# Output projection of a decoder layer as seven products of halves, on one Trainium2 core

## The chip, the core and the metric

The kernel runs on one core of a Trainium2 chip. A core has five engines with a queue of instructions each: TensorE (PE) multiplies matrices and writes to the accumulators (PSUM), VectorE (DVE) and ScalarE (ACT) work on elements, GpSimd (POOL) does so too and issues those transfers that add to their target, SyncE (SP) issues the plain loads. Each engine takes its queue in the order in which the program was built; semaphores make one engine wait for another or for a transfer. The metric is the time of one execution in device microseconds (us), as a median of several runs.

## The reference

Two decoder layers work on a stream x of 512 tokens by 1024 channels in float32. Only what the change touches is spelled out:

```python
for l in range(2):
    x = x + 0.5 * swiglu(rms_norm(x, g1[l]), wg1[l], wu1[l], wd1[l])
    h = rms_norm(x, gmix[l])
    z = h @ w_in[l]                       # q | k | v | conv_B | conv_C | conv_h
    attn_out = sliding_window_attention(q, k, v, sink[l])      # 512 x 512
    conv_out = conv_B * causal_conv3(conv_C * conv_h)          # 512 x 512
    x = x + concat([attn_out, conv_out]) @ w_out[l]            # 1024 x 1024
    x = x + 0.5 * swiglu(rms_norm(x, g2[l]), wg2[l], wu2[l], wd2[l])
return rms_norm(x, gfinal)
```

## The kernel before, in words

The stream lies transposed in four pairs of tiles (`xpair`, `xs`): 128 channels on the partitions, 512 tokens along each row. A float32 product is made of three products in a shorter float type: each operand is split into a high part, cast by ACT (`split`, line 198), and a low part, subtracted by DVE (line 199), and PE adds high x high, high x low and low x high.

Weights come through one list of units (`plan`, `add_unit`). A unit is a tile of 128 x 1024 float32 values, 512 KB. `need_raw` has SP load it (line 182) into one of 8 "raw" slots, which attention shares for its probabilities, and has POOL add a second block to it on the way in where the unit is a sum (line 193). `need_split` makes the high and low parts two groups ahead, in three buffers each. With "far" as the way (lines 236 to 238), ACT makes both the high part and a negated copy, and a transfer issued by POOL adds the raw tile to the copy, so DVE has nothing to do.

In most of the feed-forward the products run in a scheme of seven products of halves instead of eight (`seven` for the weights, `CHAINS`, `SHARES` and the class `Seven` for the operand): the weight matrix and the operand are cut in two by two, sums of the blocks are formed (the operand's are called b11, b21, t2, t3, t1, t4, b22), and seven products of half size give the result. The down projection has two such stages per feed-forward ("s"); `share` runs each: seven steps of two groups, 48 products of 128x256 per step (`stand`), and after each step two updates of a quarter of the stream on DVE (line 892). Where a norm follows, `take_half` (lines 407 to 435) makes its operands by quarters, after steps 3, 4, 5 and 6.

`mix` is the part of the layer between the feed-forwards. Eighteen groups of `w_in` give k, v, q and the conv inputs; between the groups, `attend` runs eight units of attention (scores, softmax, transposes, values). Attention results are added up by DVE (line 1217), cast by ACT (line 1221) and their low part is subtracted by POOL (line 1222); conv results are multiplied by POOL (line 1272), cast by ACT (1273), and their low part subtracted by DVE (1274). Then come eight groups of 24 products of 128x512 with `w_out` (lines 1278 to 1281), each added to one tile of the stream (1280) and handed to the next norm (`after`, lines 387 to 405).

A planner sets the order of the work on each engine when the program is built, outside the opening; the order is fixed from then on.

Of the kernel before, what the change touches and what calls it, by code (L numbers as in the profile page):

```python
# [58 lines left out]
def trunk_kernel(  # L59
# [55 lines left out]
    def f32(ap):  # L115
        return ap.bitcast(F32)
# [84 lines left out]
    def need_split(g):  # L201
        while state["split"] <= min(g, len(order) - 1):
# [3 lines left out]
            if what in (None, "wide", "far"):  # L206
                need_raw(u + LOAD_AHEAD)
                raw = raw_of.pop(u)
            elif isinstance(what, tuple):

                what, h, how = what
                far = how == "far"
                last = {"a11": 0, "a12": 4, "s2": 2, "s3": 6, "s1": 2, "a22": 8, "s4": 4}[what]
                need_raw(u + max(last, 4) + h + LOAD_AHEAD)
                a11, s1, a12, s3, a22 = (raw_of.get(u + 2 * i + h) for i in range(5))
                if what == "s2":
                    nc.vector.tensor_add(a11, a11, s1)  # L217
                raw = {"a11": a11, "a12": a12, "s2": a11, "s3": s3, "s1": s1, "a22": a22, "s4": a12}[what]
            else:

                need_raw(u + 4 + LOAD_AHEAD)
                a11, a12, s1, s3, a22 = (raw_of.get(u + i) for i in range(5))
                if what == "s2":
                    nc.vector.tensor_add(a11, a11, s1)
                if what == "s4":
                    nc.vector.tensor_add(a11, a11, a12)
                raw = {"a11": a11, "a12": a12, "s2": a11, "s3": s3, "s1": s1, "a22": a22, "s4": a11}[what]
                if what == FORMS[-1]:
                    for i in range(5):
                        del raw_of[u + i]  # L230
# [417 lines left out]
    def make_bias():  # L648
# [9 lines left out]
        for h in range(NH):  # L658
            nc.vector.scalar_tensor_tensor(
                bias[:, h, :], df, -(2.0 ** -(h + 1)), m0, op0=ALU.mult, op1=ALU.add  # L660
            )


    def ffn(norm, stages, after=None, late=None):

# [167 lines left out]

            pending.extend(lambda *tag, c=c: turn(c, *tag) for c in range(NT))

        def stand(accs, wh, wl, xh, xl, h, start):

            for c in range(4):
                cols = slice(c * P, (c + 1) * P)
                for k in range(2):  # L840
                    for i, (w, x_) in enumerate(((wh, xh), (wh, xl), (wl, xh))):

                        nc.tensor.matmul(  # L843
                            accs[c // 2][:, c % 2, :],
                            w[:, k, cols],
                            x_[:, 2 * h + k, :],
                            start=start and c % 2 == 0 and h + k + i == 0,
                            stop=h + k == 2 and i == 2,
                            skip_group_check=True,
                        )  # L850

        def stream(accs, wh, wl, xh, xl, h, start):

            for u in range(2):
                tok = slice(u * P, (u + 1) * P)
                for k in range(2):
                    for i, (x_, w) in enumerate(((xh, wh), (xl, wh), (xh, wl))):
                        nc.tensor.matmul(  # L858
                            accs[u],
                            x_[:, 2 * h + k, tok],  # L860
                            w[:, k, :],
                            start=start and h + k + i == 0,
                            stop=h + k == 2 and i == 2,
                            skip_group_check=not start,
                        )

        def share(b, ops, between, y=None):


            accs = {}  # L870
            for step, (acc, operand, start) in enumerate(CHAINS):
                ops.make(operand)
                xh, xl = ops.forms[operand]
                if start:
                    tag = {"x": "mm", "y": "sc", "w": "aux"}[acc]
                    shape = [P, 2, H] if y is None else [P, S]
                    accs[acc] = [psum(tag, shape, f"{acc}_{ops.name}_{m}") for m in range(2)]
                o, t, sign = SHARES[step]
                for h in range(2):
                    _, wh, wl = take_split()  # L880
                    if y is None:
                        stand(accs[acc], wh, wl, xh, xl, h, start)
                    else:
                        stream(accs[acc], wh, wl, xh, xl, h, start)
                    if h == 0:
                        continue
                    for m in range(2):
                        if y is None:
                            part = xpair[2 * o + m][:, :, t * H : (t + 1) * H]
                        else:  # L890
                            part = y[2 * t + m][o]
                        nc.vector.scalar_tensor_tensor(
                            part, accs[acc][m], 0.5 * sign, part, op0=ALU.mult, op1=ALU.add
                        )
                if step < 3:
                    ops.make(CHAINS[step + 4][1])
                between(step)

        def shared(b):
            return Seven([raws[b], raws[b + 2]], room_form, f"s_{norm.i}_{b}")  # L900

        def turns(step):
# [2 lines left out]
                flush()  # L905
            if step == 2:
                flush(2, "mm")

        def ahead(ops, at):
            return lambda step: ops.make(*at.get(step, ()))  # L910

        sevens = [b for what, b in stages if what == "s"]
        blocks = [b + j for b in sevens for j in (0, 2)]
# [9 lines left out]
        for i, (what, b) in enumerate(stages):  # L923
# [10 lines left out]
            if what == "s" and b == sevens[0]:  # L934
                then = shared(sevens[1])
                share(
                    b,
                    ops,
                    ahead(then, {3: ("b11",), 4: ("b21",), 5: ("t2",), 6: ("t3",)}),
                    end and end.y,  # L940
                )
            elif what == "s" and i + 1 == len(stages):
                share(b, then, after.step)
            elif what == "s":
                share(b, then, lambda step: 2 <= step < 6 and flush(1, "aux"), end and end.y)
            if what == "p":
                plain(b)
                if b == 0 and late:
# [146 lines left out]


    def mix(l, norm, after):
        mixed = [None] * KC
        q = [None] * NH

        def scaled(acc, name, by=None):
            t = g2(name)
# [11 lines left out]
        for g in range(NKV):  # L1114
# [5 lines left out]
        amix = {}  # L1120
        for g in range(NKV):
            h = parts_of(f"m_{l}_{g}")
            amix[g] = h
            for j in range(2):
                mixed[2 * g + j] = (h[0][:, j, :], h[1][:, j, :])

        def take_values():
            vf = scaled(vacc, f"vf_{l}")
# [13 lines left out]
        class Unit:  # L1142
# [61 lines left out]
            def values(self):  # L1204
# [7 lines left out]
                    nc.tensor.matmul(o, v, lo, start=False, stop=i == len(self.pt) - 1)  # L1212
# [8 lines left out]
                nc.scalar.copy(mh, f)  # L1221
                nc.gpsimd.tensor_sub(ml, f, f32(mh))

        todo = [Unit(n, g) for g in range(NKV) for n in range(NT)]

# [21 lines left out]
        for pair in range(2):  # L1247
# [6 lines left out]
            for j in range(2):  # L1254
# [11 lines left out]
                ys.append(y)  # L1266
                attend(step)
                step += 1
            hi, lo = parts_of(f"m_{l}_{2 + pair}")
            for j in range(2):  # L1270
                b = scaled(group(norm.h), f"cb_{l}_{pair}_{j}")
                nc.gpsimd.tensor_mul(b, b, ys[j])
                nc.scalar.copy(hi[:, j, :], b)
                nc.vector.tensor_sub(lo[:, j, :], b, f32(hi[:, j, :]))
                mixed[4 + 2 * pair + j] = (hi[:, j, :], lo[:, j, :])
# [62 lines left out]
```

## Time and profile before

| | |
|---|---|
| median of 3 runs | 1692.73 us (1692.41 to 1692.82) |
| the profiled execution | 1692.13 us, its span 1690.3 us |
| granted TensorE clock | 0.999 |
| PE busy | 1680.5 us, 99% of the span |
| DVE busy | 1345.3 us, 80% |
| ACT busy | 942.3 us, 56% |
| POOL busy | 209.5 us, 12% |
| projection of layer 0 | 470.2 to 513.7 us |

Times in the views are us from the start of the span, if not marked ns. A row of the timeline has the start, the duration, the engine, the line of the kernel, the operation, output <- inputs, the shape, the number of instructions merged, and in brackets how long the engine was idle before and what ended that. Durations overlap: an engine starts the next instruction before the last has left, so what an instruction costs a full queue is the distance from start to start. In the table by stretch each engine's busy time is followed by its number of instructions.

### The profile page before, as it was taken

What the parts mean: (1) busy time and instruction counts of PE and PEld (TensorE: products, weight loads), DVE (VectorE), ACT (ScalarE), POOL (GpSimd) and SP (SyncE); (2) the same over time, 40 slices, a digit from 0 to 9 for tenths busy, and PEclk for the clock granted to TensorE, in tenths of its full rate; (3) what the DMA queues carried; (4) which work ended last, traced back from release to release, by engine and by line L of the source; (5) the groups of instructions that cost most, each with busy time, mean ns of one, the idle gap of its engine ahead of it and who ended that gap; (6) DMA issues with size and microseconds to landing.
All of it is one profiled execution on the core that took longest, in us unless ns stands there. A gap on an engine that the chain in (4) does not pass through costs nothing.

```text
span 1690.3 us, 22800 instructions
## 1 busy us (share of the span) xinstructions
PE 1680.5 (99%) x8726; PEld 1434.4 (85%) x8726; DVE 1345.3 (80%) x1751; ACT 942.3 (56%) x1309; POOL 209.5 (12%) x190
## 2 busy tenths in 40 slices
PE   9999999999999999999999999999999999999998
PEld 6888899988888888889988888999888888888886
DVE  7987679988858976799798777997787597667995
ACT  6545565466535655564465555644565466556654
POOL 1011111001211111111011111110023011111111
PEclk9999999999999999999999999999999999999999
DMA  8467777731337677778576777794223457777881
GB/s 250 104 170 190 185 198 184 191 100 51 112 102 154 172 183 182 186 195 209 163 150 170 191 185 184 192 224 139 62 63 114 112 124 192 184 185 185 222 215 50
DMA packets 197600, 271.53 MB, mean 161 GB/s; under 512 B 8620, under 2 KB 91636, under 8 KB 197492
## 3 DMA queue, kind: packets, MB, share of 16 engines
q1 hardware_dynamic: 162308, 197.85, 37.5%
q0 software_dynamic: 34032, 70.79, 24.7%
q8 instruction: 68, 1.11, 0.3%
q10 hardware_dynamic: 1152, 1.45, 0.2%
q14 instruction: 40, 0.33, 0.1%
HBM read 254.85 MB, written 2.10 MB: 152 GB/s over the span
## 4 chain that ended last, share of the span: by engine, by line
PE 96%; DVE 2%; ACT 1%; DMA 0%; issue 0%; SPq 0%; ACTq 0%; DVEq 0%
PE x L858 24%; PE y L858 12%; PE acc L271 9%; PE acc L268 9%; PE acc L275 9%; PE x_s L843 8%; PE w L858 6%; PE y_s L843 4%; PE x_s L858 3%; PE w_s L843 2%; PE at L823 2%; PE y_s L858 1%; PE x L737 1%; PE w_s L858 1%; PE pt L1197 1%; DVE p L1190 0%
## 5 line engine op out<-in xcount | busy, mean ns | idle before, releaser
L198 ACT CAST wh<-raw 128x1024 fp32r<-128x1024 f32 (+1 forms) x472 | 494.7, 1048 | 552.7 <-PE x L858 134.2
L199 DVE TENSOR_TENSOR wl<-raw,wh 128x1024 fp32r<-128x1024 f32 (+1 forms) x471 | 578.5, 1229 | 214.5 <-ACT wh L198 212.5
L268 PE MATMUL acc<-xh,wh 128*128 128x512 f32 x448 | 176.5, 394 | 0.1
L271 PE MATMUL acc<-xl,wh 128*128 128x512 f32 x448 | 175.2, 391 | 0.1
L275 PE MATMUL acc<-xh,wl 128*128 128x512 f32 x416 | 162.4, 390 | 0.0
L193 POOL DMA_DIRECT2D raw<-in_ffn_wu_dram x39 | 47.3, 1217 | 569.1 <-DMA raw<-in_ffn_wu_dram 402.1
L271 PEld LDWEIGHTS acc<-xl,wh 128*128 128x128 f32 x448 | 84.2, 188 | 18.3 <-DVE xl L396 1.6
L268 PEld LDWEIGHTS acc<-xh,wh 128*128 128x128 f32 x448 | 84.2, 188 | 17.4 <-issue 0.5
L275 PEld LDWEIGHTS acc<-xh,wl 128*128 128x128 f32 x416 | 78.1, 188 | 16.3
L193 POOL DMA_DIRECT2D raw<-in_ffn_wg_dram x39 | 47.1, 1220 | 218.2 <-DMA raw<-in_ffn_wu_dram 70.9
L193 POOL DMA_DIRECT2D raw<-in_ffn_wd_dram x32 | 38.5, 1204 | 265.7 <-DMA raw<-in_ffn_wd_dram 144.8
L217 DVE TENSOR_TENSOR raw<-raw,raw 128x1024 f32<-128x1024 f32 x54 | 65.6, 1220 | 1.7 <-DMA raw<-in_ffn_wu_dram 1.0
L858 PE MATMUL w<-wh,fb21h 128*128 128x512 f32 x152 | 60.7, 399 | 0.0
L858 PE MATMUL x<-wh,ft2h 128*128 128x512 f32 x152 | 60.6, 398 | 0.0
L858 PE MATMUL y<-wh,ft3h 128*128 128x512 f32 x152 | 60.4, 398 | 0.0
L858 PE MATMUL w<-wl,fb21h 128*128 128x512 f32 x152 | 59.4, 391 | 0.0
L858 PE MATMUL x<-wl,ft2h 128*128 128x512 f32 x152 | 59.3, 390 | 0.0
L858 PE MATMUL y<-wh,ft3l 128*128 128x512 f32 x152 | 59.2, 390 | 0.0
L858 PE MATMUL y<-wl,ft3h 128*128 128x512 f32 x152 | 59.2, 390 | 0.0
L858 PE MATMUL w<-wh,fb21l 128*128 128x512 f32 x152 | 59.2, 389 | 0.0
L858 PE MATMUL x<-wl,fb11h 128*128 128x512 f32 x152 | 59.2, 389 | 0.0
L858 PE MATMUL x<-wh,fb11l 128*128 128x512 f32 x152 | 59.1, 389 | 0.0
(440 smaller groups left out, 4656.9 us busy)
## 6 DMA issues: line engine op xcount, KB each, us to landing
raw<-in_ffn_wu_dram SPq DMA_DIRECT2D x127, 512.0 KB, 4.0
raw<-in_ffn_wd_dram SPq DMA_DIRECT2D x104, 512.0 KB, 5.1
raw<-in_ffn_wg_dram SPq DMA_DIRECT2D x87, 512.0 KB, 4.5
raw<-in_ffn_wu_dram POOLq DMA_DIRECT2D x39, 512.0 KB, 7.9
raw<-in_ffn_wg_dram POOLq DMA_DIRECT2D x39, 512.0 KB, 5.9
raw<-in_w_in_dram SPq DMA_DIRECT2D x36, 512.0 KB, 3.7
raw<-in_ffn_wd_dram POOLq DMA_DIRECT2D x32, 512.0 KB, 8.1
raw<-raw POOLq DMA_DIRECT2D x16, 512.0 KB, 6.9
```

The lines of the kernel that those rows point to most:

```text
L193: nc.gpsimd.dma_start(out=r, in_=rows_of(*more), accum_op=ALU.add)
L198: nc.scalar.copy(hi, raw)
L199: eng.tensor_sub(lo, raw, f32(hi))
L217: nc.vector.tensor_add(a11, a11, s1)
L268: nc.tensor.matmul(acc, hi[:, k, :], rhs[k][0], start=k == first, stop=False)
L271: nc.tensor.matmul(acc, hi[:, k, :], rhs[k][1], start=False, stop=n == 0 and k == last)
L275: nc.tensor.matmul(acc, lo[:, k, :], rhs[k][0], start=False, stop=k == last)
L737: nc.tensor.matmul(out, w[:, k, cols], x_[:, k, :], start=start and k + i == 0, stop=k == KC // 2 - 1 and i == 2, skip_group_check=not start,)
L823: nc.tensor.transpose(tp[:, t * P : (t + 1) * P], ups[t][:, c * P : (c + 1) * P], ident)
L843: nc.tensor.matmul(accs[c // 2][:, c % 2, :], w[:, k, cols], x_[:, 2 * h + k, :], start=start and c % 2 == 0 and h + k + i == 0, stop=h + ...
L858: nc.tensor.matmul(accs[u], x_[:, 2 * h + k, tok], w[:, k, :], start=start and h + k + i == 0, stop=h + k == 2 and i == 2, skip_group_chec ...
L1197: nc.tensor.transpose(tp[:, h, :], self.p[:, h, kb * P : (kb + 1) * P], ident)
```

## The change

The output projection of each layer uses the seven products of halves in the place of eight wide groups.

- `plan` puts the `w_out` units in as one `seven` group with the new way "all" ("far" for the first block, a11). With "all" the two sums of weights (s2 and s4) are additions by transfers that POOL issues, not by DVE.
- `mixed` is two float32 tiles of 128 x 4 x 512 (attention, conv). DVE's additions of attention and POOL's conv product write to them, and the casts and subtractions that followed are gone. A `Seven` makes the forms from the two tiles: b11 after the last but one group of `w_in`, b21 after the last, the others two steps ahead of their use (`soon`).
- `share`, `stand`, `stream` and `ahead` move out of `ffn`, unchanged but for the factor `by` and `soon`.
- The second norm of the layer takes the stream by quarters (`after.step`), as the norm behind the first feed-forward of layer 0 does.

```diff
@@ need_split
-                if what == "s2":
+                if what == "a12" and how == "all":
+                    nc.gpsimd.dma_start(out=a11, in_=s1, accum_op=ALU.add)
+                if what == "s2" and how != "all":
                     nc.vector.tensor_add(a11, a11, s1)
...
-                if what == "s3" and how == "share":
+                if what == "s3" and how in ("share", "all"):
                     nc.gpsimd.dma_start(out=a12, in_=a11, accum_op=ALU.add)
@@ plan
-            cols(w_out[l], 0, KC, KC)
+            seven(
+                lambda o, j, h: (w_out[l], KC // 2 * j + 2 * h, 2, o * S, S),
+                lambda what, h: "far" if what == "a11" else "all",
+            )
@@ share (moved out of ffn)
+                if soon and step + 2 < len(CHAINS):
+                    ops.make(CHAINS[step + 2][1])
                 for m in range(2):
...
                     nc.vector.scalar_tensor_tensor(
-                        part, accs[acc][m], 0.5 * sign, part, op0=ALU.mult, op1=ALU.add
+                        part, accs[acc][m], by * sign, part, op0=ALU.mult, op1=ALU.add
                     )
-            if step < 3:
+            if not soon and step < 3:
                 ops.make(CHAINS[step + 4][1])
@@ mix
-        mixed = [None] * KC
+        mixed = [g8(f"m_{l}_{j}", F32, (P, KC // 2, S)) for j in range(2)]
+        ops = Seven(mixed, room_g8, f"m_{l}")
...
-                f = g2(f"of_{self.name}", F32, (P, 2, P))
+                f = mixed[0][:, 2 * g : 2 * g + 2, n * P : (n + 1) * P]
...
-                mh, ml = (z[:, :, n * P : (n + 1) * P] for z in amix[g])
-                nc.scalar.copy(mh, f)
-                nc.gpsimd.tensor_sub(ml, f, f32(mh))
...
-                nc.gpsimd.tensor_mul(b, b, ys[j])
-                nc.scalar.copy(hi[:, j, :], b)
-                nc.vector.tensor_sub(lo[:, j, :], b, f32(hi[:, j, :]))
+                nc.gpsimd.tensor_mul(mixed[1][:, 2 * pair + j, :], b, ys[j])
...
-        for c in range(KC):
-            acc = group(mixed)
-            nc.vector.tensor_add(xs[c], acc, xs[c])
-            after(c)
+                if step == 17:
+                    ops.make("b11")
+        ops.make("b21")
+        share(ops, 1.0, after.step, soon=True)
```

More of the change, by code (lines that the diff above doesn't have):

```diff
@@ new lines, in stream @@
+    def stream(accs, wh, wl, xh, xl, h, start):
+        for u in range(2):
+            tok = slice(u * P, (u + 1) * P)
+            for k in range(2):
+                for i, (x_, w) in enumerate(((xh, wh), (xl, wh), (xh, wl))):
+                    nc.tensor.matmul(
+                        accs[u],
+                        x_[:, 2 * h + k, tok],
+                        w[:, k, :],
+                        start=start and h + k + i == 0,
+                        stop=h + k == 2 and i == 2,
+                        skip_group_check=not start,
+                    )
@@ new lines, in share @@
+    def share(ops, by, between, y=None, soon=False):
+        accs = {}
+        for step, (acc, operand, start) in enumerate(CHAINS):
+            ops.make(operand)
+            xh, xl = ops.forms[operand]
+            if start:
+                tag = {"x": "mm", "y": "sc", "w": "aux"}[acc]
+                shape = [P, 2, H] if y is None else [P, S]
+                accs[acc] = [psum(tag, shape, f"{acc}_{ops.name}_{m}") for m in range(2)]
+            o, t, sign = SHARES[step]
+            for h in range(2):
+                _, wh, wl = take_split()
+                if y is None:
+                    stand(accs[acc], wh, wl, xh, xl, h, start)
+                else:
+                    stream(accs[acc], wh, wl, xh, xl, h, start)
+                if h == 0:
+                    continue
+                if soon and step + 2 < len(CHAINS):
+                    ops.make(CHAINS[step + 2][1])
+                for m in range(2):
+                    if y is None:
+                        part = xpair[2 * o + m][:, :, t * H : (t + 1) * H]
+                    else:
+                        part = y[2 * t + m][o]
+                    nc.vector.scalar_tensor_tensor(
+                        part, accs[acc][m], by * sign, part, op0=ALU.mult, op1=ALU.add
+                    )
+            if not soon and step < 3:
+                ops.make(CHAINS[step + 4][1])
+            between(step)
@@ L664, in ffn, with ahead @@
+    def ahead(ops, at):
+        return lambda step: ops.make(*at.get(step, ()))
     def ffn(norm, stages, after=None, late=None):
@@ L834, in winograd2 @@
             pending.extend(lambda *tag, c=c: turn(c, *tag) for c in range(NT))
[L836 to L865, printed above, removed]
@@ L942, in ffn @@
             elif what == "s" and i + 1 == len(stages):
-                share(b, then, after.step)
+                share(then, 0.5, after.step)
             elif what == "s":
-                share(b, then, lambda step: 2 <= step < 6 and flush(1, "aux"), end and end.y)
+                share(then, 0.5, lambda step: 2 <= step < 6 and flush(1, "aux"), end and end.y)
             if what == "p":
```

52 lines of the change are left out of this document (14 added, 38 removed).

## The prediction

> **What bounds the kernel now.** I read the page first, then the table of waits of TensorE, then the busy time of each engine by stretch, and last the timelines around the output projection of layer 0.
>
> ```profile
> PE 1680.5 (99%) x8726; PEld 1434.4 (85%) x8726; DVE 1345.3 (80%) x1751; ACT 942.3 (56%) x1309; POOL 209.5 (12%) x190
> ...
> PE 96%; DVE 2%; ACT 1%; DMA 0%; issue 0%; SPq 0%; ACTq 0%; DVEq 0%
> ```
>
> TensorE (PE) is busy for 99% of the span and carries 96% of the chain that ended last, so a product taken away is time taken away, as long as nothing makes PE wait. In the attention it waits already, a little, for VectorE (DVE):
>
> ```profile
> PE o L1212 <- DVE pl L1201: 0.8, 2, 0.4
> ```
>
> The stretches below are the output projection of layer 0, and the last product of halves of the first feed-forward (its second "s" stage), which has the form that the projection is to get.
>
> ```profile
> core 0: us, PE busy (x) PEld busy (x) DVE busy (x) ACT busy (x) POOL busy (x), PEclk, DMA share, GB/s
> 470.20:513.70 43.50, 43.50 (x193) 36.03 (x192) 25.31 (x30) 17.06 (x23) 2.68 (x3) 1.00 0.34 92
> 309.30:349.60 40.30, 40.30 (x337) 40.30 (x337) 36.29 (x51) 24.20 (x35) 1.76 (x2) 1.00 0.65 170
> ```
>
> The projection leaves DVE 18 of 43.5 us free. The product of halves leaves it 4 of 40.3. That DVE time, not the saved products, decides this case.
>
> **The change part by part. Fewer products.** First and last of the 192 wide products of layer 0, and the next stage's first:
>
> ```profile
> 470.22 0.39 PE L268 MATMUL acc<-m,wh 128*128 128x512 f32 x1
> ...
> 513.51 0.39 PE L275 MATMUL acc<-m,wl 128*128 128x512 f32 x1
> 513.74 0.39 PE L268 MATMUL acc<-xh,wh 128*128 128x512 f32 x1
> ```
>
> The pace is 43.29 / 191 = 0.2267 us, and the stage costs 43.5. In the chain, a step of the existing product of halves (48 products of 128x256) reads:
>
> ```profile
> 750.84 5.76 PE w_s L843 x48
> 756.60 5.76 PE x_s L843 x48
> ```
>
> That is 0.120 us each. Seven steps cost 7 x 5.76 = 40.3 us. Saved: 3.2 us a layer, 6.4 in all. That is less than an eighth, since a half-width product costs 53% of a wide one.
>
> **The attention ahead of it.** Results now go to float32 tiles straight from the additions, so the casts L1221 and L1273, the subtractions L1274 on DVE and L1222 on GpSimd (POOL) go. In their place ScalarE (ACT) casts "b11" and DVE subtracts it, between the last unit's maxima and its exponentials. Around there:
>
> ```profile
> 452.34 0.22 DVE L1186 TENSOR_TENSOR sums<-sums,es 128x4 f32<-128x4 f32 x1 [1.17 <-ACT es L1185]
> 455.66 1.29 DVE L1201 TENSOR_TENSOR pl<-pt,ph 128x512 fp32r<-128x512 f32 x2
> 457.29 0.39 PE L1212 MATMUL o<-pl,vv 128*128 128x512 f32 x1
> ```
>
> DVE's gap of 1.17 us takes most of the 1.14 us, but the conv scaling behind it moves 0.8 us, with it POOL's product and ACT's tap. In the new order the tap stands before both "pl", and the weights' subtraction between them. I get the second "pl" at 458.0 against PE's need at 457.29: 0.7 us of wait. The subtraction L1274 that is gone saves 0.2 of the earlier wait. Net +0.5 us; bounds 0 (the gap takes it all) and 1.5 (a whole weight subtraction more). The stage then begins at 470.8.
>
> **POOL's queue.** New on POOL per layer are 4 adding loads, 2 transfers that finish the split of "a11", and 4 additions of one weight tile to another; 8 subtractions like the one below go. SP issues 10 loads for 8; by the count of DVE's queue further down, the two that wait for a tile's slot (a22) can go at about 484, land after the 4.0 us below and are wanted at 498, so they are hidden. The next feed-forward's first weights likewise: their slot comes free at 489, and they are cast at 505. If that cover were gone, each would cost its 4 us once.
>
> ```profile
> 469.63 0.74 POOL L1222 TENSOR_TENSOR m<-of,m 128x256 fp32r<-128x256 f32 x1 [2.34 <-ACT m L1221]
> ```
>
> ```profile
> L238 POOL DMA_DIRECT2D wl<-raw x9: 852/889/901, 527.4 to 1373.0; - x9
> ...
> DMA to landing us min/median/max: 4.4/5.3/9.1
> ```
>
> ```profile
> L193 POOL DMA_DIRECT2D raw<-in_ffn_wu_dram x39: 1194/1203/1423, 32.8 to 1530.8; - x39
> ...
>   DMA raw<-in_ffn_wu_dram: 473.0, 39
> ```
>
> ```profile
> raw<-raw POOLq DMA_DIRECT2D x16, 512.0 KB, 6.9
> raw<-in_w_out_dram SPq DMA_DIRECT2D x16, 512.0 KB, 4.0
> ```
>
> POOL stands still until an earlier transfer has landed (473 us over the span). So far little was queued behind such a wait. In the new order the last conv product (cb x y, needed by "b21") stands behind one:
>
> ```profile
> 463.83 1.05 ACT L198 CAST wh<-raw 128x1024 fp32r<-128x1024 f32 x1 [0.36 <-PE acc L271]
> 465.08 2.21 POOL L1272 TENSOR_TENSOR cb<-cb,cc 128x512 f32<-128x512 f32 x1 [0.73 <-DVE cb L1104]
> 471.26 1.29 POOL L1272 TENSOR_TENSOR cb<-cb,cc 128x512 f32<-128x512 f32 x1 [0.89 <-DVE cb L1104]
> ```
>
> ACT casts the second half of a11 when PE gives a buffer free: 463.83 + 0.6, two passes of 1.05, ready at 466.6. POOL: the other conv product until 467.5; issue of the transfer; an adding load of 1.2 until 469.6; then the addition to raw_98, which waits for that transfer. It lands 5.9 us after 467.5 (I take a value between the two medians 5.3 and 6.9, because three transfers are issued within 4 us): 473.4. Issue 0.9, product 1.3: 475.5, where before it was 472.6. With 4.4 it is 474.1, with 9.1 it is 478.8. DVE's next item, the difference t3, waits for it with everything behind, so DVE stands from 472.4 to 475.5.
>
> **DVE's queue.** Its pace, from the end of the existing product of halves:
>
> ```profile
> 348.81 1.22 DVE L199 TENSOR_TENSOR wl<-raw,wh 128x1024 fp32r<-128x1024 f32 x1
> 349.95 0.42 DVE L431 TENSOR_TENSOR nacc<-nacc,nsq 128x256 f32<-128x256 f32 x1
> 350.28 0.69 DVE L892 SCALAR_TENSOR_TENSOR x<-x_s,x 128x512 f32<-128x512 f32 x1
> 350.88 0.42 DVE L432 TENSOR_TENSOR nacc<-nacc,nsq 128x256 f32<-128x256 f32 x1
> 351.21 0.69 DVE L892 SCALAR_TENSOR_TENSOR x<-x_s,x 128x512 f32<-128x512 f32 x1
> 351.82 0.87 DVE L421 SCALAR_TENSOR_TENSOR xl<-x,par,xh 128x256 fp32r<-128x256 f32 x2
> ```
>
> Start to start: 1.14 us for 1024 columns, 0.60 for an update of the stream, 0.40 for a quarter's low half, 0.33 for a sum of squares. From t3 to the last two updates the new program has on DVE 13 weight subtractions, 6 of forms and 4 sums (23 x 1.14 = 26.2), 12 updates (7.3), 12 quarters (4.8) and 8 sums of squares (2.7): 41.0 us, against 18 wide items in the existing stage:
>
> ```profile
> L199 DVE TENSOR_TENSOR wl<-raw,wh 128x1024 fp32r<-128x1024 f32 x14 | 17.1, 1222 | 3.7 <-ACT wh L198 3.7
> ```
>
> There 3.7 us were idle, waiting for casts; here there are five wide items more (5.7 us) and the late start. The queue reaches the last two updates at 475.5 + 41.0 = 516.5, where PE alone would have ended the stage at 511.1. Two updates, two sums and a low half later, at 518.9, the next norm's group gets its 14th product's operand (order 4 to 7, then 0 to 3). 13 x 0.2267 = 2.95 before that is its start as far as PE can tell: 515.95, 4.85 after 511.1. PE meets this in pieces (for "b21" in step 1, for weights in steps 5 and 6, for the first low halves). ACT was busy for 24.2 us in the existing stage and gets two wide passes more, about 26 of 40, so it is no bound.
>
> **Behind it** the reciprocal root comes late by as much, and the stage that follows is a full DVE queue:
>
> ```profile
> 535.84 0.68 DVE L199 TENSOR_TENSOR a<-gate,a 128x512 fp32r<-128x512 f32 x1
> 535.98 0.84 PE L268 MATMUL acc<-a,wh 128*128 128x512 f32 x3
> 536.44 0.68 DVE L683 TENSOR_TENSOR gate<-acc,gate 128x512 f32<-128x512 f32 x1
> ```
>
> In the new order the first low half of "a" stands behind the second gate's product, not before: 0.5 us more (0 to 1).
>
> Sum per layer: -3.2 + 0.5 + 4.85 + 0.5 = +2.65, for two layers +5.3. The profiled execution took 1692.13 (span 1690.3), so 1697.4; the median of the runs is 0.6 above it, and I carry that over: 1698.
>
> **Where a page would give another sum.** Rows: 4.4, 5.3 and 9.1 us from issue to landing. The Trainium skill, "DMA: Bandwidth & Descriptors", section "Anatomy of one DMA — SWDGE (gpsimd) path", gives 2.0 us plus bytes over 436e3, an estimate of 3.2 us for 512 KB. By that the product would be done at 473.0 and the sum would be about +0.3 per layer. None of the nine rows is that short, and these transfers add rather than copy, so I go by the rows. The next rival is this case, worked out as a mechanism.
>
> **The rivals.**
> 1. *Early landing, no change.* The transfer's landing does not hold POOL: the product runs once its operand is scaled (471.75) and ends at 473.0. DVE then ends 2.4 us earlier, the group starts at 513.5, the layer gains or loses 0.3: about 1693. For it: DMA share is only 0.34 in this stage. Against: the shortest row is 4.4, and three transfers come together.
> 2. *The saving arrives whole, faster.* DVE keeps step and PE loses nothing: 1692.7 - 6.4 = 1686.3. For it: the existing stage ran 90% full on DVE with its first closing update 0.7 us after PE. It decides if the queue reaches the closing updates before about 512, 4.5 us earlier than counted: product at 472.6 as now, and some 1.5 us less work. Against: five wide items more than that stage.
> 3. *Landing at the slow end.* 9.1 us puts DVE 3.3 us later again, both layers +6.6: 1704.
>
> **How the numbers follow.** 0.2% is 3.4 us and about what a measurement tells from no change. Forecast (1696.1 to 1702, slower): 0.45. Rival 3: 0.12. Rival 1 (1689.3 to 1696.1): 0.24. Rival 2: 0.19. Faster 0.19, same 0.24, slower 0.57. The range 1687 to 1703 leaves out half of rivals 2 and 3 each, 0.16; the forecast's own is 1695 to 1702.
>
> **What would show it.** Right: in the new trace 48-product steps of about 5.8 us with stretched ones in the first two and last two; POOL's last L1271 of a layer waiting for a DMA and ending about 475; DVE idle before t3 some 3 us, and then nearly full to the next norm; PE waits named fb21 or wl and xl at the stage's end. Wrong: POOL's product at 473, or DVE with gaps in the stage (then rival 2), or PE waits that lie in the attention instead.

## The result and the profile after

The changed kernel took 1708.24 us (median of 5 runs, 1707.49 to 1710.53) where the kernel before took 1692.56 (1692.41 to 1692.82): a ratio of 1.0095, 95% interval 1.008 to 1.011. It is slower by 15.7 us. The prediction said 1698.0 with a range of 1687 to 1703; the direction was right, the size was not, and the time lies outside the range.

The profiled execution took 1710.53 us, the longest of the five; its span is 1708.8 and its mean granted clock 0.995 (0.999 before). On its page, the busy time of the engines and the shares of the chain that ended last:

```profile
PE 1682.7 (98%) x9014; PEld 1447.4 (85%) x9014; DVE 1380.9 (81%) x1815; ACT 964.5 (56%) x1331; POOL 214.4 (13%) x194
...
PE 90%; DVE 4%; DMA 3%; issue 2%; POOL 1%; ACT 1%; POOLq 0%; DVEq 0%; ACTq 0%; SPq 0%
```

PE's busy time is longer, although the projection issues fewer product columns, and its share of the chain fell from 96% to 90%. Transfers, which had 0% of the chain, have 3%. What PE waits for now (total, times, longest):

```profile
PE x_m L675 <- DMA wl<-raw: 11.2, 2, 5.6
PE acc L277 <- DVE wl L199: 2.0, 2, 1.0
...
PE o L1215 <- DVE pl L1204: 1.1, 2, 0.7
PE x L690 <- DMA wl<-raw: 0.9, 1, 0.9
PE acc L270 <- ACT xh L425: 0.8, 2, 0.4
PE y_m L675 <- DVE wl L199: 0.6, 2, 0.3
```

The first row is new and is by far the largest: once per layer PE stands for 5.6 us, waiting for the transfer that finishes a split weight. The busy time by stretch shows where, and what follows it (columns as in the table by stretch above; the last three are the granted clock, the DMA share and GB/s):

```profile
470.60:473.70 3.10, 3.10 (x27) 3.05 (x25) 1.92 (x2) 1.01 (x1) 1.03 (x1) 1.00 1.07 202
473.70:479.40 5.70, 0.15 (x2) 0.00 (x0) 0.00 (x0) 0.00 (x0) 0.00 (x0) 0.84 1.07 206
479.40:484.40 5.00, 4.93 (x23) 4.93 (x24) 2.45 (x3) 1.99 (x3) 3.04 (x3) 0.50 0.84 163
...
481.90:519.50 37.60, 37.29 (x301) 37.09 (x300) 37.55 (x51) 26.26 (x36) 1.70 (x3) 0.97 0.66 175
```

From 473.7 to 479.4 no engine works, but for the end of PE's last products; only transfers run. In the next 5 us PE is busy, but at half the clock (0.50): it starts 23 products, where a step at full clock starts 42 in that time (5.00 / 0.120). From 481.9 to the end of the stage DVE is busy for 37.55 of 37.60 us.

The same place instruction by instruction, from the timelines of layer 0:

```profile
467.26 0.89 POOL L217 DMA_DIRECT2D raw<-raw  x1
467.85 1.61 POOL L1271 TENSOR_TENSOR m<-cb,cc 128x512 f32<-128x512 f32 x1
469.09 1.22 POOL L240 DMA_DIRECT2D wl<-raw  x1
...
479.47 0.58 PE L675 MATMUL x_m<-fb11h_m,wl 128*128 128x256 f32 x1 [5.62 <-DMA wl<-raw]
...
479.72 0.89 POOL L217 DMA_DIRECT2D raw<-raw  x1 [8.09 <-DMA wl<-raw]
480.30 1.61 POOL L1271 TENSOR_TENSOR m<-cb,cc 128x512 f32<-128x512 f32 x1
...
481.95 1.23 DVE L510 TENSOR_TENSOR sums_m<-m,m 128x1024 f32<-128x1024 f32 x1 [9.08 <-POOL m L1271]
483.09 1.22 DVE L199 TENSOR_TENSOR fb21l_m<-m,fb21h_m 128x1024 fp32r<-128x1024 f32 x1
...
522.78 0.69 DVE L726 SCALAR_TENSOR_TENSOR x<-x_m,x 128x512 f32<-128x512 f32 x1
```

The transfer for the second half of a11 is issued at 469.09 and lands at 479.43. Two things wait for it: PE, in the middle of step 0, and POOL, whose next entry (L217) overwrites the tile that the transfer reads. The other L217, at 467.26, is the same addition for the first half; it was issued ahead of the late transfer and runs beside it. Behind the L217 at 479.72 stands the last conv product, and behind the product DVE's whole queue, idle for 9.08 us.

Where the time went, by the starts of the same products in the profiled executions. "Stage" is from the first product of the projection to the first of the next feed-forward's gate, "norm" from there to that feed-forward's first product of halves, "x step" the first such step in layer 1's first feed-forward, whose code the change does not touch. All in us; the kernels from e1 on are the experiments below.

| kernel | stage, layers 0 / 1 | norm, layers 0 / 1 | x step |
|---|---|---|---|
| before | 43.52 / 43.52 | 33.39 / 33.38 | 5.44 |
| after | 48.92 / 48.85 | 36.44 / 36.42 | 6.62 |
| e1 | 41.79 / 41.09 | 36.38 / 36.38 | 6.50 |
| e2 | 41.10 / 41.36 | 36.40 / 36.39 | 6.58 |
| e3 | 48.71 / 48.55 | 35.48 / 35.55 | 6.52 |
| e5 | 48.21 / 48.47 | 36.41 / 36.39 | 6.66 |
| e6 | 41.54 / 40.79 | 38.06 / 39.67 | 9.21 |
| e7 | 52.70 / 51.88 | 34.14 / 34.13 | 5.53 |
| e8 | 48.43 / 46.91 | 34.52 / 35.63 | 10.11 |
| e10 | 41.55 / 41.12 | 34.71 / 34.76 | 8.03 |
| e11 | 40.94 / 41.76 | 37.22 / 36.12 | 5.79 |
| e12 | 41.87 / 42.17 | 35.45 / 35.45 | 5.44 |

After against before: 10.7 in the two stages, 6.1 in the two norms, 1.2 in the x step, together 18.0 of the 18.5 us by which the spans differ. The rest lies in the opening and the attention.

### The profile page after: what moved, and what is told of

It reads as the page before. It is cut to its first block, busy times and chain, and to the rows that moved or that the text cites. A ratio compares the mean times of both kernels' runs of the same rounds, so it can differ in the third digit from the quotient of the medians.

```text
span 1708.8 us, 23557 instructions
## 1 busy us (share of the span) xinstructions
PE 1682.7 (98%) x9014; PEld 1447.4 (85%) x9014; DVE 1380.9 (81%) x1815; ACT 964.5 (56%) x1331; POOL 214.4 (13%) x194
## 3 DMA queue, kind: packets, MB, share of 16 engines
q10 hardware_dynamic: 1152, 1.45, 0.2%
## 4 chain that ended last, share of the span: by engine, by line
PE 90%; DVE 4%; DMA 3%; issue 2%; POOL 1%; ACT 1%; POOLq 0%; DVEq 0%; ACTq 0%; SPq 0%
PE x L690 24%; PE y L690 12%; PE x_s L675 8%; PE acc L273 7%; PE acc L270 6%; PE w L690 6%; PE acc L277 6%; PE y_s L675 4%; PE x_s L690 3%; PE w_s L675 2%; PE at L896 2%; DMA wl<-raw 1%; PE y_s L690 1%; DVE wl L199 1%; PE x_m L675 1%
## 5 line engine op out<-in xcount | busy, mean ns | idle before, releaser
L198 ACT CAST wh<-raw 128x1024 fp32r<-128x1024 f32 (+1 forms) x480 | 502.9, 1048 | 530.0 <-PE x L690 133.7
L199 DVE TENSOR_TENSOR wl<-raw,wh 128x1024 fp32r<-128x1024 f32 (+1 forms) x479 | 586.0, 1225 | 208.6 <-ACT wh L198 206.9
```

Source lines behind the costliest of these rows:

```text
L198: nc.scalar.copy(hi, raw)
L199: eng.tensor_sub(lo, raw, f32(hi))
```

## The experiments

All are edits of the changed kernel. Four questions: is the late transfer the cause (e1, e2, e3, e5), what is the half clock worth (e7), is what is left DVE's queue (e6, e8, e10), and can it be given to transfers (e11, e12).

**e1: no transfer for a11.**

```diff
-                lambda what, h: "far" if what == "a11" else "all",
+                lambda what, h: "all",
```

> Edit: both halves of a11 are split like every other weight, cast by ACT and subtracted by DVE; the two transfers that finished the split of a11 are gone, DVE has two wide items more per layer. Theory A (the landing of the transfer for the second half is what costs): TensorE no longer pauses in step 0 (5.7 us per layer) and the half-speed products behind the pause go (about 2 us per layer), so about 15 us less than the changed kernel, some 1693, if DVE hides its two items. Rival B (DVE's queue is the limit anyway, as the prediction had it): DVE has 43.3 us of work from about 472.6, reaches the closing updates at about 516, and the kernel takes about 1697 to 1699, with the waits at the end of the stage. Rival C (not the split but the loads behind the busy DMA queues are late): TensorE still waits for a transfer in the first two steps and the time stays above 1703.

Measured: 1696.63 us, ratio to the kernel before 1.0024 (1.0015 to 1.0033). The wait on the transfer is gone and so is the slow stretch: the stage takes 41.8 and 41.1 us in the place of 48.9. That is 11.6 us back, so theory A names the larger part, and C falls. But the time is 1696.6, next to B's 1697 to 1699, and not 1693: the norm still takes 36.4 us, 3.0 more than before.

**e2: a transfer for the first half of a11 only.**

```diff
+                lambda what, h: "far" if (what, h) == ("a11", 0) else "all",
```

> Edit: only the first half of a11 is finished by a transfer; the second half is subtracted by DVE. Theory A: the second half alone was late, so the pause in step 0 goes here too; one wide DVE item less than with both halves on DVE, so the same time as that kernel or up to 2 us less: 1691 to 1693. Rival B: 1696 to 1698, between that kernel and the prediction. Rival C: above 1703.

Measured: 1695.71 us, ratio 1.0016 (1.0007 to 1.0026). The second half alone was late. The time lies just under B's 1696 to 1698 and above A's 1691 to 1693. The two largest waits of PE behind the opening, DVE's share from its late start to the end of the stage, and the two ends of DVE's queue:

```profile
PE acc L277 <- DVE wl L199: 1.9, 2, 1.0
...
PE x L690 <- DMA wl<-raw: 0.8, 1, 0.8
```

```profile
473.60:511.10 37.50, 37.16 (x308) 36.84 (x308) 37.49 (x51) 26.25 (x36) 1.75 (x2) 1.00 0.77 194
```

```profile
473.61 1.23 DVE L510 TENSOR_TENSOR sums_m<-m,m 128x1024 f32<-128x1024 f32 x1 [1.25 <-POOL m L1271]
...
514.44 0.68 DVE L726 SCALAR_TENSOR_TENSOR x<-x_m,x 128x512 f32<-128x512 f32 x1
```

DVE is busy for 37.49 of 37.50 us, at a granted PE clock of 1.00. From its first difference to the last updates it takes 514.44 - 473.61 = 40.83 us, exactly as long as in the changed kernel (522.78 - 481.95 = 40.83). The stage itself gains 2.4 and 2.2 us and the norm loses 3.0 each time.

**e3: the last conv product on DVE.** This takes the product out from behind POOL's wait and leaves the transfer as it is.

```diff
-                nc.gpsimd.tensor_mul(mixed[1][:, 2 * pair + j, :], b, ys[j])
+                eng = nc.vector if pair and j else nc.gpsimd
+                eng.tensor_mul(mixed[1][:, 2 * pair + j, :], b, ys[j])
```

> Edit: the last conv product of each layer runs on DVE, not on POOL behind the addition that waits for the transfer. Theory A (TensorE itself waits for the transfer, POOL's hold is second): the pause of about 5.7 us per layer in step 0 stays, DVE starts on t3 some 9 us earlier and the waits at the end of the stage and in the next norm's groups shrink, 1 to 2.5 us per layer: 1703 to 1706. Rival (the prediction's step: the product held on POOL, with DVE behind it, is what costs): the product is ready at 473 and the time falls to 1693 or less.

Measured: 1707.08 us, ratio 1.0084 (1.0069 to 1.0099). PE's waits and the stretch:

```profile
PE x_m L675 <- DMA wl<-raw: 10.5, 2, 5.3
```

```profile
472.90:478.40 5.50, 0.26 (x3) 0.06 (x1) 4.36 (x4) 1.03 (x1) 0.00 (x0) 0.72 1.06 192
478.40:481.00 2.60, 2.58 (x12) 2.58 (x13) 0.03 (x1) 0.00 (x0) 1.78 (x2) 0.50 0.94 176
```

DVE now works during the pause (4.36 us), and PE stands all the same, then runs at half clock. PE's own need of the transfer is enough to cost the stage its time; the prediction had only seen the path through POOL and DVE. Only 1.2 us come back, most of it in the norm (35.5 in the place of 36.4).

**e5: the sums s2 on DVE.** The two additions of one weight tile to another by transfers (L217) go. Only the first of them runs beside the late transfer; in the changed kernel the second is issued at 479.72, behind the landing.

```diff
-                lambda what, h: "far" if what == "a11" else "all",
+                lambda what, h: "far" if what == "a11" else "share",
```

> Edit: both halves of a11 keep their transfers, but the sum s2 = a11 + s1 is formed by DVE, as in the feed-forward, not by two more transfers. Theory D (the landing is long because four transfers share the same engines: 10.3 us at 205 GB/s are about four times 512 KB): with the two additions gone the transfer of the second half lands about 2.5 us sooner, 7 to 8 us after its issue, and TensorE pauses some 3 us per layer in the place of 5.7; POOL's last product no longer stands behind the wait. DVE takes two wide items more. About 1702 to 1704. Rival E (the landing is long for a reason of its own, whatever runs beside it): 10 us again, the pause stays at 5 to 6 us and the time is 1706 to 1710.

Measured: 1709.33 us, ratio 1.0099 (1.0084 to 1.0114), no better than the change. The landing (least, median, most; the one transfer of the second half in layer 0), first of the changed kernel, then of e5, and then e5's timeline:

```profile
DMA to landing us min/median/max: 10.3/10.3/10.3
```

```profile
DMA to landing us min/median/max: 6.3/6.3/6.3
```

```profile
476.17 1.23 DVE L219 TENSOR_TENSOR raw<-raw,raw 128x1024 f32<-128x1024 f32 x1 [6.95 <-DMA wl<-raw]
477.31 0.68 DVE L1113 TENSOR_TENSOR cb<-acc,inv 128x512 f32<-128x512 f32 x1
...
478.14 2.12 POOL L1271 TENSOR_TENSOR m<-cb,cc 128x512 f32<-128x512 f32 x1 [6.01 <-DVE cb L1113]
```

Theory D holds for the landing: it is 4 us shorter with one transfer less beside it, and PE's pause is 2.39 us. In layer 1 the difference is smaller, 5.9 us against 8.6. Its forecast of the time fails. DVE's addition now waits for the same transfer, the scaling of the conv operand stands behind it in DVE's queue, and the product behind that: it ends at 480.3, where the changed kernel has 481.9. The queue that is held up has changed, not the time.

**e7: PE kept busy during the wait.** 48 products into an accumulator that nobody reads.

```diff
+                if spin and step == 0 and h == 1:
+                    idle = psum("aux", [P, 2, H], f"idle_{ops.name}")
+                    for i in range(spin):
+                        nc.tensor.matmul(
+                            idle[:, 0, :], wh[:, 0, :P], xh[:, 0, :], start=True, stop=True, ...
```

> Edit: 48 products of 128x256 on operands that are ready, into a spare accumulator that nobody reads, between the two halves of step 0, 5.8 us of TensorE work in the place of the 5.7 us of standing still. Theory A1 (the granted clock of 0.50 for 4.9 us is set off by TensorE standing still): the clock stays at 1.00, the 22 products behind the wait run 0.120 us apart instead of 0.213, and 2 us per layer are saved: about 1704. Rival (the clock falls because of something else in that stretch, the transfers for example): the half clock shows again and the time is 1708 to 1710.

Measured: 1712.94 us, ratio 1.0119 (1.0104 to 1.0134): slower than the change, where A1 expected 4 us less. The stretches and the waits of PE:

```profile
474.10:480.00 5.90, 5.90 (x52) 5.90 (x51) 0.00 (x0) 0.00 (x0) 0.65 (x2) 1.00 1.06 203
480.00:482.90 2.90, 2.90 (x26) 2.86 (x24) 1.30 (x2) 1.05 (x1) 2.41 (x3) 1.00 0.87 171
482.90:491.00 8.10, 3.80 (x27) 3.21 (x26) 8.10 (x8) 4.84 (x5) 0.00 (x0) 1.00 0.38 75
491.00:495.00 4.00, 4.00 (x21) 4.00 (x22) 4.00 (x5) 1.79 (x2) 0.85 (x1) 0.57 0.66 131
```

```profile
PE w_m L675 <- ACT wh L198: 4.1, 2, 2.0
PE w_m L675 <- DVE wl L199: 2.6, 2, 1.3
PE w_m L675 <- DVE fb21l_m L199: 1.3, 2, 0.9
```

A1's cause holds: with PE busy, the clock stays at 1.00 through the same transfers (DMA share 1.06), and the 24 products behind take 2.9 us. Its price does not. PE arrives sooner at step 1 and waits there for fb21's low part, which comes from the late product, so the half clock was hidden behind that. The other two waits, 3.4 us a layer, come from the order of the program: with 48 products more on PE, the planner put the forms ahead of step 1's weights on ACT and DVE. So e7 does not price the clock. The trace of the changed kernel does: fb21's low part is done at 483.09 + 1.22 = 484.31 and the first product that reads it runs at 484.48, so with DVE this late a full clock would have saved at most 0.2 us.

**e6: the norm by whole tiles (on e2).** `take` and `square` on four tiles after step 5 and four after step 6, in the place of the quarters.

```diff
+            for c in {5: range(4, 8), 6: range(4)}.get(step, ()):
+                self(c)
...
-            part = {3: (0, 0), 4: (1, 1), 5: (1, 0), 6: (0, 1)}.get(step)
```

> Edit: on the same kernel, the second norm takes the stream by whole tiles, four after step 5 and four after step 6, not by quarters after steps 3 to 6. DVE's total falls by about 1.5 us (8 wide low parts of 0.68 in the place of 16 quarters), but more of it stands behind the last updates. Theory (the quarters bring DVE's work ahead of the end): four wide low parts and four sums behind the last update take about 4.5 us where the quarters take 2.5, so 1 to 2.5 us per layer slower: 1698 to 1701. Rival (the queue's length alone counts): 1 to 1.5 us per layer faster, 1693 to 1694.

Measured: 1700.97 us, ratio 1.0052 (1.0037 to 1.0068), 5.3 more than e2. The norm takes 38.1 and 39.7 us, 1.7 and 3.3 more than e2; the x step in layer 1, 2.6 more, lies in code that this edit does not touch, and why it is longer was not followed. The profiled execution (1702.42 us) was 1.5 slower than the median. The quarters are worth having in this form of the stage.

**e8: four low parts per layer on POOL (on e2).** In e2 POOL is idle from 480 to 515.

```diff
+LIGHT = [(what, 1, "all") for what in ("s3", "s1", "a22", "s4")]
...
+                split(hi, lo, raw, nc.gpsimd if own else nc.vector)
```

> Edit: on the kernel with only the first half of a11 finished by a transfer, the low parts of the second halves of s3, s1, a22 and s4 are subtracted by POOL, which has nothing to do in that stretch (0.00 us busy from 480 to 515). Theory B (what is left of the loss is DVE's queue, full from 473.6 to 522): 4 x 1.14 = 4.6 us less on DVE per layer, the waits at the end of the stage (0.5 + 1.1 + 0.5 + 0.4 us) go, and the time falls by 4 to 5 us against 1695.7, to about 1691. Rival (those waits are the length of the closing chain from the last update through low parts and root, not the queue before it): less than 1.5 us is gained, 1694.5 to 1696.

Measured: 1705.26 us, ratio 1.0072 (1.0055 to 1.0089), 9.6 more than e2; neither theory. Three of POOL's subtractions and DVE's rows beside them:

```profile
487.99 2.85 POOL L200 TENSOR_TENSOR wl<-raw,wh 128x1024 fp32r<-128x1024 f32 x1 [8.08 <-ACT wh L199]
494.03 3.03 POOL L200 TENSOR_TENSOR wl<-raw,wh 128x1024 fp32r<-128x1024 f32 x1 [3.19 <-ACT wh L199]
498.79 2.59 POOL L200 TENSOR_TENSOR wl<-raw,wh 128x1024 fp32r<-128x1024 f32 x1 [1.73 <-ACT wh L199]
```

```profile
489.08 2.85 DVE L517 TENSOR_TENSOR sums_m<-sums_m,m 128x1024 f32<-128x1024 f32 x1
...
494.71 3.42 DVE L200 TENSOR_TENSOR ft4l_m<-sums_m,ft4h_m 128x1024 fp32r<-128x1024 f32 x1
...
498.66 3.00 DVE L428 SCALAR_TENSOR_TENSOR xl<-x,par,xh 128x256 fp32r<-128x256 f32 x2
```

Beside a POOL subtraction a DVE item takes 2.85 to 3.42 us where it takes 1.22 (or 0.87, the last). The first two end 1.1 us after POOL's (491.93 and 490.84, 498.13 and 497.06): DVE does its work when POOL is done. So each of the three cost DVE about 2 us for 1.14 us of work taken away. PE then waited 3.7 us once in each layer for a weight that DVE had to split (y_m <- DVE wl), and in layer 0 its granted clock was 0.50 from 504.6 to 510.5. How much of the 9.6 us each part has was not taken apart. The theory on the queue was not tested by this run.

**e10: four low parts per layer left out (on e2).** The same four subtractions are left out of the computation; PE multiplies by the high part in the place of the low one, so its work is the same.

```diff
+            lo = hi if bare else wpool.tile(shape, F32R, tag="wl", bufs=3, name=f"wl_{n}")
```

> Edit: on the kernel with only the first half of a11 finished by a transfer, the low parts of the second halves of s3, s1, a22 and s4 are left out of the computation; TensorE multiplies by the high part in their place, so it does the same number of products, and DVE has 4 items of 1.14 us less per layer. Theory B (the waits behind the stage are DVE's queue): 4.6 us less queue per layer removes the 3.0 us of waits at the end of the stage and in the next norm's groups, about 6 us less than 1695.7: 1689 to 1691, so faster than the kernel before by the saved products. Rival (the closing chain from the last update through low parts to the norm's last product sets those waits, whatever stands in the queue before): less than 2 us is gained, 1694 to 1696.

Measured: 1691.44 us, ratio 0.9993 (0.9984 to 1.0002). The waits on weights behind the stage are gone; among the rows left:

```profile
PE x L694 <- DMA wl<-raw: 2.3, 1, 2.3
PE w_m L679 <- DVE fb21l_m L200: 1.5, 2, 0.9
```

By the medians it is 4.3 us less than e2, most of the 6 us of theory B and more than the rival's 2. The profiled executions differ by only 1.3 us (1693.31 and 1694.59): e10's is the slowest of its ten, with an x step 1.45 us longer than e2's. In them the norm falls only to 34.7 us: of its 3.0 us over the kernel before, 1.7 are the queue, and 1.3 are left with 4.6 us less to do. Those I have not taken apart.

**e11 and e12: DVE items given to transfers (on e2).** In both, the addition that forms t4 is a transfer. In e11 the low part of the next feed-forward's second gate group is one too. In e12 it is not; instead the first feed-forward of layer 1 splits its first weight of the stage that follows on DVE.

```diff
-                    nc.vector.tensor_add(self.sums[1], self.sums[1], b21)
+                    nc.gpsimd.dma_start(out=self.sums[1], in_=b21, accum_op=ALU.add)
@@ e11, plan of the next feed-forward's gate and up groups
+                    how = "far" if (w is wu, j) in far else None
@@ e12, plan of layer 1's first feed-forward
-                        lambda what, h: "far" if (b, what, h) == (1, "a11", 0) else None,
+                        lambda what, h: "far" if (b, what, h) == (1, "a11", 0) and not near else None,
```

> Edit: on the same kernel, two DVE items of 1.14 us per layer become transfers in a stretch in which POOL has nothing to do: the addition that forms t4, and the low part of the second gate group of the next feed-forward. Theory B: 2.3 us less queue per layer, so 2 to 4 us less than 1695.7 in all: 1691.5 to 1693.5, about the kernel before. Rival F (a transfer lands 6 to 10 us later and something waits for it in its turn): t4 or the gate's low part comes late, TensorE waits, above 1695.

> Edit: on the kernel with only the first half of a11 finished by a transfer, the addition that forms t4 is a transfer (1.14 us off DVE per layer), and in the first feed-forward of layer 1 the first weight of the second stage is split by DVE, not by a transfer that POOL issues behind an adding load. Theory B: the end of the projection gains about 1 us per layer; theory G (the wait of 0.8 to 1.2 us at the head of that stage, which the kernel before does not have, is POOL's order there): that wait goes. Together 3 us less than 1695.7, about 1692.5, no better than the kernel before, since DVE still has about 40 us of work in a stage of 40.3. Rival: t4's transfer or DVE's extra item in layer 1 costs as much as is gained, 1695 to 1696.

Measured: e11 1698.35 us, ratio 1.0035 (1.0021 to 1.0048); e12 1693.50 us, ratio 1.0004 (0.9995 to 1.0013). In e11 the rival was right: PE waits for the gate's transfer.

```profile
PE acc L277 <- DMA wl<-raw: 3.3, 2, 2.2
```

In e12 the x step is back at 5.44, which is theory G. With t4 by a transfer the norm gains 0.95 us, and the stage loses 0.8 in each layer, so that part is worth nothing. e12 is the best form found that computes everything: level with the kernel before, not better.

## Why the prediction was wrong, by its steps

**Fewer products, -3.2.** Right. The steps run at 5.76 us wherever nothing waits, and e2's stage takes 41.1 us against 43.5.

**The attention, +0.5.** Too large. The second "pl" is waited for by 0.7 us, as said, but the kernel's earlier wait for a "pl" is gone. The stage begins at 470.58 against 470.22, and in layer 1 the stretch from the end of the x step to the stage takes 416.98 us against 417.06. Call it 0 to 0.3.

**POOL's queue.** This is the step that failed. Its mechanism was right: the last product stands behind a wait for the transfer, and DVE behind the product. Its size was not. "Lands 5.9 us after 467.5" was 10.33 us after 469.09 in layer 0, and t3, expected at 475.5, started at 481.95. The issue came late because an adding load ahead of it in POOL's queue waited for its plain load; the chain of waits in the changed kernel shows both transfers:

```profile
458.94 6.46 DMA raw<-in_w_out_dram
...
469.09 10.33 DMA wl<-raw
```

The landing lies outside the bounds of 4.4 to 9.1 us, which were rows from other places of the program. In layer 1 it took 8.6 us, inside those bounds, but there the issue came behind the stage's first product (1315.06 against 1314.88), where in layer 0 it came 1.5 us ahead of it. The DMA share here is 1.07; the 0.34 that rival 1 went by was the old stage's, from 470 on, and the new program brings more transfers to just this place. In e5, with one transfer less beside it, the landing was 4 us shorter. The fit of the Trainium skill ("DMA: Bandwidth & Descriptors", "Anatomy of one DMA — SWDGE (gpsimd) path"), an estimate of 3.2 us for 512 KB, was further off: the shortest of these rows in either kernel is the 4.4 that the prediction showed.

Put into the prediction's own sum, the measured start of t3 is 6.45 us later than the expected one, so a layer loses 2.65 + 6.45 = 9.1 us, and 1692.13 + 18.2 = 1710.3 for the profiled execution, which took 1710.53. This one term accounts for the miss. That it does so to 0.2 us is partly luck: the attention's term was too large by 0.7 us in all, and the x step below, 1.2 us, was not in the sum.

What the prediction did not see at all is a second path, because it never asked when PE itself wants that tile. The last product that can do without it starts at 473.57, so PE wants it at 473.69. With my 473.4 that is in time by 0.3 us, and every later landing stops PE. In layer 0 the pause and the slow products behind it cost PE 8.0 us (10.76 us from 473.57 to 484.33, for 23 products of 0.120). This runs beside DVE's late start and is not added to it; either is enough for most of the loss in the stage. Without the late product (e3) the stage is still 48.7 us, and with PE's pause cut to 2.39 us (e5) it is still 48.2. e1 and e2, which take away both, bring it to 41 to 42 us. Rival 3 had the direction, but counted its landing of 9.1 us from 467.5, and priced only the path through DVE.

**DVE's queue, 41.0 us.** Right to 0.2 us, in two kernels: 40.83. With e2's start at 473.6 in the place of 475.5 its reading gives 2.95 + 0.5 us behind the end of PE's own work, the gate's 0.5 us included; e2 loses 0.8 in the stage and 3.0 in the norm. So once the transfer is in time this part of the sum holds: e1, where PE waits for no landing in this stage, is at 1696.6, inside the forecast's own range of 1695 to 1702. That DVE's time decides was true of this stage: it is why e1 and e2 do not pay even without the pause, and with four DVE items left out (e10) the time falls by 4.3 us.

**Not in the sum: the x step of layer 1, +1.2.** The change does not touch this code. In the kernel before, then in the changed one, POOL's queue and the chain:

```profile
871.69 1.21 POOL L193 DMA_DIRECT2D raw<-in_ffn_wg_dram  x1 [2.66 <-DMA raw<-in_ffn_wu_dram]
873.61 0.90 POOL L238 DMA_DIRECT2D wl<-raw  x1 [0.71 <-DVE sums L505]
```

```profile
871.54 6.15 DMA wl<-raw
877.74 5.88 DMA raw<-in_ffn_wu_dram
...
884.93 7.79 DMA wl<-raw
892.77 2.35 PE x L690 x9
```

The transfer is issued at 884.93, 11.3 us later than before, where PE's work there comes 8.85 us later (891.28 against 882.43 for the step's first product): an adding load in front of it waits for its plain load, which started late. e12 takes this transfer away and the step is 5.44 us again. The chain shows what is ahead of it: the plain load starts when an earlier transfer of the same kind, issued at 871.54, has landed. In the kernel before, that transfer took 4.7 us in the place of 6.15 and the plain load behind it 3.6 in the place of 5.88. Why these two landings are longer was not followed further.

**The signs.** Of what the prediction named as signs, the 48-product steps, DVE full to the next norm and POOL's product behind a DMA wait are there. The product ended at 481.9 and not at 475, DVE stood for 9.1 us before t3 and not for 3; and the table of PE's waits is led by a transfer, which it had not named.

## What to carry to other kernels

Where a step hands work to a transfer, write down three times for it: when its queue really gets to issue it, how long it lands in the traffic that the new program has at that place, and when the earliest reader wants it. A landing taken from other stretches was 3 to 4 us too short here. If the slack is shorter than the spread of the rows, the reader's pause is to be priced as a path of its own, beside the one that is already in the sum. Where two paths wait for the same landing, taking one away gains little while the other stays (e3, e5), and an engine that is idle is not a free place if it slows the one that is to be relieved (e8).

## What the runs showed of the hardware that I had not expected

- **Half clock after a pause.** With the pause of 5.6 us PE's granted clock fell to 0.50: it was 0.84 in the mean over the pause and 0.50 for about 5 us behind it, where 128x256 products ran 0.213 us apart in the place of 0.120. It is not the traffic: in e7 the clock stayed at 1.00 under the same transfers while PE was busy, and fell to 0.57 behind two pauses of 2.0 and 1.3 us. The length of the pause alone does not tell: in e6 one of 2.42 us (536.1 to 538.6) left the clock at 1.00, and one of 1.86 us (885.6) was followed by 0.50, which held on where no transfer ran any more (the second row):

```profile
538.60:541.00 2.40, 2.23 (x10) 1.73 (x11) 2.25 (x3) 1.70 (x3) 0.80 (x1) 1.00 1.02 148
...
890.00:892.00 2.00, 2.00 (x6) 1.52 (x6) 0.00 (x0) 0.66 (x1) 0.00 (x0) 0.50 0.00 0
```

  What does tell is how the pause lies in a fixed grid. In each trace the changes of the granted clock lie whole multiples of 3.41 us apart (477.56 and 484.38 in the changed kernel, 888.72 and 892.14 in e6). In e6 the pause of 1.86 us lies inside one cell of that grid, while of the 2.42 us no cell has more than 1.62. Counted so over all the traces, from 60 us to the end of PE's work, a cell at full clock with 1.86 us or more of idle time was followed by half clock each time, and one with 1.62 or less never; between them, 1.75 us was (e5) and 1.77 was not (e10). This is read off the traces, and no run was made to test it.

  The Trainium skill, "TensorE: Matmul & The Clock Gate", section "Part 1: The HAM clock gate (the "warmup" mystery)", has two states, full and half, and a window of about 3.4 us that runs freely, so that the same pause can fall into it in more ways than one. The two states and the window agree with these rows. The same section of the Trainium skill ties half clock to at least one idle window of that length; here 1.86 us of idle time in one cell were enough.
- **POOL stops DVE.** Beside a POOL subtraction of 2.6 to 3.0 us, DVE items with two inputs in SBUF took 2.85 to 3.42 us and finished only behind it (e8). The Trainium skill, "SBUF — State Buffer", section "SBUF: two separate sides", says that the two engines share a pair of ports that one of them holds for a whole instruction; these rows agree.
- **A transfer of 512 KB that adds to its target** landed in 10.3 us in the changed kernel and in 6.3 us at the same place in e5, which has one such transfer less beside it (8.6 and 5.9 us in layer 1).
